# Layer 0's last stage in a written order: last gate group, first GLA weights and norm

## The chip, the cores and the metric

The kernel runs on one core of a Trainium2 chip, as one program. The profile names the core's engines: PE (matrix products, with PEld loading its weights), DVE and ACT (element-wise work), POOL, and SP, from which most loads are issued. ACT and POOL issue loads too. Each engine works through its own instructions in order, and waits on semaphores for the others.

The metric is the time of one execution in device microseconds. Times given are medians of several runs.

## The reference, cut to what matters

Two layers on 512 tokens of width 1024, in float32. Each has a mixer, a gated MLP and a per-layer embedding; layer 0's mixer is attention with a short convolution, layer 1's is gated linear attention (GLA). The change lies where layer 0 ends and layer 1 begins:

```python
def _rms_norm(x, gain):
    y = xf * lax.rsqrt(jnp.mean(xf * xf, axis=-1, keepdims=True) + RMS_EPS)
    return y * gain

def _per_layer_embedding(x, p_i, norm, w_gate, w_proj):   # end of layer 0
    gate = jax.nn.sigmoid(_rms_norm(x, norm) @ w_gate)
    return gate * (p_i @ w_proj)                          # added to x

def _gla_mixer(h, w_in, w_gate_up, gate_bias, o_norm, w_out):   # h = _rms_norm(x, mix_norm[1])
    q, k, v, g_lr, og = _split(h @ w_in, GLA_SPLITS)
    log_a = jax.nn.log_sigmoid(g_lr @ w_gate_up + gate_bias) / GLA_GATE_NORMALIZER
    ...
    o = _gla_chunked(heads(q) * GLA_DK ** -0.5, heads(k), heads(v), heads(log_a))
    o = _rms_norm(o, o_norm) * jax.nn.silu(heads(og))
    return o.reshape(b, s, GLA_VAL_DIM) @ w_out
```

## The kernel before

**Layout and arithmetic.** The state x is held transposed in eight tiles `xT[0..7]` of 128 features by 512 tokens. For float32 accuracy, each operand of a large product is split in two: a rounded part (made on ACT by a copy) and the rest (made on DVE by subtraction). A product is then three matmuls: rounded by rounded, and twice rounded by rest. `cut` (L134) does this for weights: `wh` on ACT at L151, `wl` on DVE at L153, or at L158 when other work is recorded between them (`amid`). `mm3_rests_last` (L181) issues for all terms first the two matmuls that need only one operand's rest, and afterwards, in a second pass, the matmul with the other operand's rest.

**End of layer 0, `ple0` (L1382).** The gate product is done in four groups g of 256 output columns, each from seven block products of half size (`product`) that share weights differences (`first_third`, `second`, `fourth` on DVE). PE, DVE and ACT follow a written order here (`manual_schedule`, L1460). A group's gate is finished one group late (`late`): a multiplication by the token norm R, a sigmoid on ACT, a multiplication by the projection of p (`pjb`, L1524, read from a PSUM bank), and an addition to `xT` (`added`, L1449). `enter` (L1412) then makes the split operands of layer 1 (`xg`: x times the gain, rounded on ACT at L113, its rest on DVE at L114), and `squared` (L1451) takes squares on ACT and adds them up in `acc` on DVE (L319). Behind the last group come the weights of the first 368 GLA value columns, in two halves `raws` (L1552 to L1563), the last gate, the last four blocks of x, and `end_norm` (L361): PE turns `acc` (L358), DVE sums it (L367) and scales it (L205), POOL takes the power -1/2 (L206).

**Start of layer 1, `mixer1` (L1752).** `v.step(0)` and `v.step(1)` (L1773) are the value product with those weights, over blocks 0 to 3 and 4 to 7 of x, into four PSUM banks of the kind `ps`. Their results are scaled by the norm when ACT evicts them (L1787, L1788). Sixteen of the columns feed the decay gate: `gate_up` (L1838) loads its weights from ACT's queue and splits them, `turn_low` (L1852) turns the columns, `log_decays` (L1865) makes the log decays on PE, ACT and DVE. `spread` (L371) turns the norm into a tile R for features in rows. `query(w, 0)` (L1806) is the first feature product, also in a `ps` bank, with `turn_low` recorded after six of its eight terms. Its weights (`pair_w`, L1792) are 1 MB, loaded by SP and split by `cut`. The masks of the chunked attention come by one load (L2093) into a weight buffer (`raw`, two buffers in all), and DVE casts them to bytes (L2094).

**What sets the order.** Outside the written stretches a scheduler orders each engine's instructions when the program is built, by priority; `issue_after(i)` keeps what is recorded in it behind instruction i, `high_priority(offset)` moves it ahead. SP's loads stand in one queue. A tile of a pool with n buffers waits until the tile n places before it has been read.

Of the kernel before, what the change touches and what calls it, by code (L numbers as in the profile page):

```python
# [19 lines left out]
P = 128  # L20
S = 512
# [42 lines left out]
class Kernel:  # L64
# [116 lines left out]
    def mm3_rests_last(self, terms, start, stop, weights, **kw):  # L181


        mm = self.nc.tensor.matmul
        begun, left = set(), {}
        for out, lt, rt in terms:
            left[id(out)] = left.get(id(out), 0) + 1
        for out, (lh, ll), (rh, rl) in terms:
            first = start and id(out) not in begun
            begun.add(id(out))  # L190
            mm(out, lh, rh, start=first, stop=False, **kw)  # L191
            lt, rt = (lh, rl) if weights == 0 else (ll, rh)
            mm(out, lt, rt, start=False, stop=False, **kw)  # L193
        for out, (lh, ll), (rh, rl) in terms:
            left[id(out)] -= 1
            lt, rt = (ll, rh) if weights == 0 else (lh, rl)
            end = mm(out, lt, rt, start=False, stop=stop and not left[id(out)], **kw)  # L197
        return end

    def rsqrt(self, out, src, scale):  # L200

        nc = self.nc
        w = src.shape[1]
        t = self.few(w, "rs", 4)
        nc.vector.tensor_scalar(t, src, scale, EPS, op0=ALU.mult, op1=ALU.add)  # L205
        nc.gpsimd.tensor_tensor(out, t, self.mhalf[:, :w], ALU.pow)  # L206

# [153 lines left out]
    def end_norm(self, sums=None):  # L361

        nc = self.nc
        if sums is None:
            ps = self.by_token()
            sums = self.few(NT, "ss")
            nc.vector.tensor_reduce(sums, ps.rearrange("p (t f) -> p t f", f=P), op=ALU.add, axis=AX.X)  # L367
        self.r = self.few(NT, "rtok")
        self.rsqrt(self.r, sums, 1.0 / D)
# [1012 lines left out]
    def ple0(self, fp, both, gain, next_gain):  # L1382
# [29 lines left out]
        def enter(*ms):  # L1412
            for m in ms:
                hl = self.pair(self.fp, "b0", "b1")
                self.split(hl, self.xT[m], next_gain[:, m : m + 1])
                self.xg.append(hl)

# [25 lines left out]
        def sigmoid(s):  # L1443
            nc.scalar.activation(s, s, AF.Sigmoid)
# [15 lines left out]
        with tc.manual_schedule(engines={ET.PE, ET.DVE, ET.Activation}):  # L1460
# [6 lines left out]
            rounded = lambda hl, src, w=S: nc.scalar.activation(hl[0][:, :w], src[:, :w], AF.Copy)  # L1467
            rest = lambda hl, src, w=S: tt(hl[1][:, :w], src[:, :w], hl[0][:, :w].bitcast(F32), ALU.subtract)
            tt(s34[:, left], e[:, left], e[:, right], ALU.subtract)
            rounded(eh, e, H)  # L1470
            rounded(oh, o)
            tt(s12[:, left], e[:, right], o[:, right], ALU.add)
            rest(eh, e, H)
            tt(s12[:, right], s12[:, left], e[:, left], ALU.subtract)
            rounded(ah, s12)
            rest(oh, o)
            rest(ah, s12)
# [3 lines left out]
            copies(X, Y, bank)  # L1481
            tt(s34[:, right], o[:, left], s12[:, right], ALU.subtract)
# [5 lines left out]
            for g in range(groups):  # L1488
# [18 lines left out]
                copy(X[:, right], Y[:, left])  # L1507
                if late:
                    summed(gates[:, 1], Yb, mb)
# [8 lines left out]
                if not ends:  # L1518
                    raw, ev, od = following
                    plain = self.cut_blocks(raw[:, :, :P])  # L1520
                if late:
                    sigmoid(gates[:, 1])
                    for c in range(2):
                        tt(gates[:, c], gates[:, c], pjb[c], ALU.mult)  # L1524
                if not ends:
                    first_third(ev, od)
                product(X[:, right], t13, 1, x["s3"], False, g > 0)
                copy(Y[:, right], X[:, right])
                if ends:
                    added(before, gates)  # L1530
                    pjs.append(proj(2 * g + 1))
                    squared(before)
                    enter(0, 1, 2, 3)
# [33 lines left out]
        self.end_norm()  # L1567
# [184 lines left out]
    def mixer1(self):  # L1752
        nc, a, tc = self.nc, self.a, self.tc
        xg, r = self.xg, self.r
        w_in = a["gla_w_in"][0].rearrange("(k p) n -> p k n", p=P)
        tok = lambda k, t: (xg[k][0][:, t * P : (t + 1) * P], xg[k][1][:, t * P : (t + 1) * P])
        with tc.tile_pool(name="m1", bufs=1) as mp:
# [5 lines left out]
            class Values:  # L1763
# [9 lines left out]
                def step(v, i):  # L1773
# [15 lines left out]

            qT, kT = [None] * GH, [None] * GH  # L1790
# [4 lines left out]
            def feature(w, c, amid=None):  # L1795
                ps = self.ps()
# [305 lines left out]
            R = self.spread()  # L2102
            w = pair_w(0)
            query(w, 0, turn_low)
# [126 lines left out]
```

## Time and profile before

| | us |
|---|---|
| median of 3 runs | 1208.24 (1206.25 to 1208.59) |
| the profiled execution | 1207.74 |
| its span, first to last instruction | 1206.0 |
| PE busy in the span | 1189.8 |
| DVE busy | 995.2 |
| ACT busy | 692.8 |
| granted PE clock, mean | 0.996 |

A row of a timeline gives the start and the duration in us from the span's start, then engine, line, operation, out<-in with their shapes, the count of merged instructions, and in brackets how long the engine was idle before it and what ended that. A row of the waits gives who waited for whom: us in total, times, longest. A row of windows gives the length of a stretch, then the busy time of PE, weight load, DVE, ACT and POOL with their counts, the granted clock of PE (1.00 is full), the share of the DMA engines and GB/s. L12 is line 12 of the kernel; a helper's line stands for all who call it.

### The profile page before, as it was taken

What the parts mean: (1) busy time and instruction counts of PE and PEld (TensorE: products, weight loads), DVE (VectorE), ACT (ScalarE), POOL (GpSimd) and SP (SyncE); (2) the same over time, 40 slices, a digit from 0 to 9 for tenths busy, and PEclk for the clock granted to TensorE, in tenths of its full rate; (3) what the DMA queues carried; (4) which work ended last, traced back from release to release, by engine and by line L of the source; (5) the groups of instructions that cost most, each with busy time, mean ns of one, the idle gap of its engine ahead of it and who ended that gap; (6) DMA issues with size and microseconds to landing.
All of it is one profiled execution on the core that took longest, in us unless ns stands there. A gap on an engine that the chain in (4) does not pass through costs nothing.

```text
span 1206.0 us, 20223 instructions
## 1 busy us (share of the span) xinstructions
PE 1189.8 (99%) x8218; PEld 1081.3 (90%) x8218; DVE 995.2 (83%) x1593; ACT 692.8 (57%) x1137; POOL 45.9 (4%) x64
## 2 busy tenths in 40 slices
PE   9999999999999999999799999999999999999998
PEld 8877789999999889889688988889999999888887
DVE  6786687898999986989769876687989999988595
ACT  7466556656565654755563565555565656645374
POOL 2600000000000000000100000000000000000000
PEclk9999999999999999999899999999999999999999
DMA  7232222333332433222231322223333333423601
GB/s 222 74 100 74 73 88 71 110 102 109 103 106 88 156 123 97 97 70 86 89 93 47 94 71 70 87 70 106 106 106 106 102 109 96 140 88 97 207 2 70
DMA packets 112928, 117.76 MB, mean 98 GB/s; under 512 B 2840, under 2 KB 107858, under 8 KB 112836
## 3 DMA queue, kind: packets, MB, share of 16 engines
q1 hardware_dynamic: 112000, 115.88, 29.8%
q8 instruction: 64, 1.05, 0.4%
q0 software_dynamic: 560, 0.42, 0.3%
q14 instruction: 28, 0.23, 0.1%
q10 hardware_dynamic: 276, 0.18, 0.1%
HBM read 114.37 MB, written 2.10 MB: 97 GB/s over the span
## 4 chain that ended last, share of the span: by engine, by line
PE 85%; DVE 10%; ACT 3%; issue 1%; DMA 1%; POOL 0%; ACTq 0%; DVEq 0%; POOLq 0%
PE ps L177 8%; PE ps L178 8%; PE ps L179 8%; PE pa L179 6%; PE pa L178 6%; PE pa L177 6%; PE ps L912 5%; PE ps L914 5%; PE ps L913 5%; PE ps L191 4%; PE ps L193 4%; PE ps L197 4%; PE pa L912 2%; PE pa L914 2%; PE pa L913 2%; DVE wl L860 1%
## 5 line engine op out<-in xcount | busy, mean ns | idle before, releaser
L153 DVE TENSOR_TENSOR wl<-raw,wh 128x1024 fp32r<-128x1024 f32 (+4 forms) x140 | 160.8, 1151 | 38.4 <-ACT wh L151 34.9
L151 ACT ACTIVATE wh<-raw 128x1024 fp32r<-128x1024 f32 (+4 forms) x142 | 140.8, 996 | 70.0 <-PE ps L178 28.5
L857 ACT ACTIVATE wh<-raw 128x1024 fp32r<-128x1024 f32 x90 | 95.7, 1064 | 127.5 <-DVE raw L884 79.8
L975 DVE SCALAR_TENSOR_TENSOR zt<-z,vfa,zt 128x510 f32<-128x510 f32 (+1 forms) x176 | 131.1, 746 | 0.3
L860 DVE TENSOR_TENSOR wl<-raw,wh 128x1024 fp32r<-128x1024 f32 x90 | 110.1, 1223 | 18.8 <-ACT wh L857 17.9
L179 PE MATMUL pa<-b,wl 128*128 128x256 f32 x352 | 97.3, 276 | 0.1
L179 PE MATMUL pa<-a,wl 128*128 128x256 f32 x352 | 97.3, 276 | 0.0
L177 PE MATMUL pa<-b,wh 128*128 128x256 f32 x352 | 97.2, 276 | 0.0
L178 PE MATMUL pa<-a,wh 128*128 128x256 f32 x352 | 97.2, 276 | 0.0
L177 PE MATMUL pa<-a,wh 128*128 128x256 f32 x352 | 97.2, 276 | 0.0
L178 PE MATMUL pa<-b,wh 128*128 128x256 f32 x352 | 97.2, 276 | 0.0
L191 PE MATMUL ps<-b,wh 128*128 128x512 f32 (+1 forms) x200 | 77.6, 391 | 5.9 <-ACT wh L151 5.9
L973 ACT ACTIVATE zt<-z,vfb 128x512 f32<-128x512 f32 x88 | 71.4, 811 | 18.2 <-DVE z L965 8.8
L193 PE MATMUL ps<-b,wh 128*128 128x512 f32 (+1 forms) x200 | 76.2, 384 | 0.0
L179 PEld LDWEIGHTS pa<-b,wl 128*128 128x128 f32 x352 | 66.1, 188 | 0.3 <-DVE wl L153 0.3
L178 PEld LDWEIGHTS pa<-a,wh 128*128 128x128 f32 x352 | 66.1, 188 | 0.0
L178 PEld LDWEIGHTS pa<-b,wh 128*128 128x128 f32 x352 | 66.1, 188 | 0.0
L177 PEld LDWEIGHTS pa<-b,wh 128*128 128x128 f32 x352 | 66.1, 188 | 0.0
L177 PEld LDWEIGHTS pa<-a,wh 128*128 128x128 f32 x352 | 66.1, 188 | 0.0
L179 PEld LDWEIGHTS pa<-a,wl 128*128 128x128 f32 x352 | 66.1, 188 | 0.0
L912 PE MATMUL ps<-four,wh 128*128 128x256 f32 x232 | 64.6, 279 | 0.0
L914 PE MATMUL ps<-four,wl 128*128 128x256 f32 x232 | 64.1, 276 | 0.0
(530 smaller groups left out, 3708.6 us busy)
## 6 DMA issues: line engine op xcount, KB each, us to landing
raw<-in_ffn_w_up_dram SPq DMA_DIRECT2D x42, 1024.0 KB, 5.0
raw<-in_ffn_w_down_dram SPq DMA_DIRECT2D x13, 1024.0 KB, 5.1
raw<-in_hy_w_in_dram SPq DMA_DIRECT2D x8, 1024.0 KB, 5.2
raw<-in_gla_w_in_dram SPq DMA_DIRECT2D x8, 1024.0 KB, 5.1
raw<-in_ffn_w_down_dram SPq DMA_DIRECT2D x8, 768.0 KB, 4.8
raw<-in_ple_w_gate_dram SPq DMA_DIRECT2D x6, 1024.0 KB, 5.6
raw<-in_hy_w_out_dram SPq DMA_DIRECT2D x16, 256.0 KB, 4.2
raw<-in_gla_w_out_dram SPq DMA_DIRECT2D x4, 1024.0 KB, 5.0
```

What stands on the lines that cost most here:

```text
L151: nc.scalar.activation(hv, v, AF.Copy)
L153: self.rest_cut = nc.vector.tensor_tensor(lv, v, hv.bitcast(F32), ALU.subtract)
L177: mm(out, lh, rh, start=start, stop=False, **kw)
L178: mm(out, lh, rl, start=False, stop=False, **kw)
L179: mm(out, ll, rh, start=False, stop=stop, **kw)
L191: mm(out, lh, rh, start=first, stop=False, **kw)
L193: mm(out, lt, rt, start=False, stop=False, **kw)
L857: nc.scalar.activation(h, src, AF.Copy)
L860: nc.vector.tensor_tensor(l, src, h.bitcast(F32), ALU.subtract)
L912: mm(out, wh, xh, start=first and j == 0, stop=False, **kw)
L914: mm(out, wl, xh, start=False, stop=j == ND // 2 - 1, **kw)
L975: nc.vector.scalar_tensor_tensor(out=y[:, tap:], in0=z[:, : S - tap], scalar=w[:, f : f + 1], in1=y[:, tap:], op0=ALU.mult, op1=ALU.add,)
```

## The change

In the compiled program the instructions of PE, SP, POOL, DVE and ACT before layer 0's last stage are the same. What the edit does:

- *First group.* The sum form of the first pair (`ah`) is rounded, and its rest taken, in two halves, the second behind the copies.
- *Middle groups.* The multiplication of the first gate half by its projection stands ahead of the rest of the next plain weights.
- *Last group.* `enter` is divided in `rounded_x` (ACT) and `rest_x` (DVE), and `squared` in `square` (ACT) and `sums` (DVE). Blocks 0 and 1 are rounded ahead of the second sigmoid, blocks 2 to 7, the squares, the last gate and the additions in two written lists, between the roundings and the rests of each half of the value weights.
- *Norm.* `end_norm` is issued after the first pass of `v.step(1)`, where the scheduler put the transposes in the middle of that pass before; `rsqrt` returns its DVE instruction.
- *First query.* Its weights are issued after that instruction, its product takes a `pa` bank, and `spread` is recorded with `turn_low` after six of the eight terms.
- *Masks.* Two loads into tiles of the kind `sq`, with two casts.

In the program as built, SP has the first mask load between the two loads of value weights; ACT has both roundings of the first query weights directly behind the last rounding of x and ahead of the five loads of the gate weights, and the two roundings of the first key weights ahead of L1872; on DVE the orders in the first half of layer 1 differ too (one scan, L1898, stands later). PE has the same instructions; the transposes named here, R's and the turned columns' stand elsewhere. From the third head of layer 1 on the orders are as before.

```diff
@@ -181 +181 @@
-    def mm3_rests_last(self, terms, start, stop, weights, **kw):
+    def mm3_rests_last(self, terms, start, stop, weights, amid=None, **kw):
@@ -193 +193,4 @@
-            mm(out, lt, rt, start=False, stop=False, **kw)
+            end = mm(out, lt, rt, start=False, stop=False, **kw)
+        if amid:
+            with self.tc.issue_after(end.ins), self.tc.high_priority(offset=200):
+                amid()
@@ -205 +208 @@
-        nc.vector.tensor_scalar(t, src, scale, EPS, op0=ALU.mult, op1=ALU.add)
+        scaled = nc.vector.tensor_scalar(t, src, scale, EPS, op0=ALU.mult, op1=ALU.add)
@@ -206,0 +210 @@
+        return scaled
@@ -369 +373 @@
-        self.rsqrt(self.r, sums, 1.0 / D)
+        self.norm_scaled = self.rsqrt(self.r, sums, 1.0 / D)
@@ -1412 +1416 @@
-        def enter(*ms):
+        def rounded_x(*ms):
@@ -1415 +1419 @@
-                self.split(hl, self.xT[m], next_gain[:, m : m + 1])
+                nc.scalar.activation(hl[0], self.xT[m], AF.Copy, scale=next_gain[:, m : m + 1])
@@ -1417,0 +1422,17 @@
+        def rest_x(*ms):
+            for m in ms:
+                h, l = self.xg[m]
+                nc.vector.scalar_tensor_tensor(
+                    out=l, in0=self.xT[m], scalar=next_gain[:, m : m + 1], in1=h.bitcast(F32),
+                    op0=ALU.mult, op1=ALU.subtract,
+                )
+        def square(m):
+            sq = spare()
+            nc.scalar.activation(sq, self.xT[m], AF.Square)
+            return sq
+        def sums(*sqs):
+            for sq in sqs:
+                tt(self.acc, self.acc, sq, ALU.add)
@@ -1467,2 +1488,3 @@
-            rounded = lambda hl, src, w=S: nc.scalar.activation(hl[0][:, :w], src[:, :w], AF.Copy)
-            rest = lambda hl, src, w=S: tt(hl[1][:, :w], src[:, :w], hl[0][:, :w].bitcast(F32), ALU.subtract)
+            whole = slice(0, S)
+            rounded = lambda hl, src, c=whole: nc.scalar.activation(hl[0][:, c], src[:, c], AF.Copy)
+            rest = lambda hl, src, c=whole: tt(hl[1][:, c], src[:, c], hl[0][:, c].bitcast(F32), ALU.subtract)
@@ -1470,2 +1492 @@
-            rounded(eh, e, H)
-            rounded(oh, o)
+            rounded(eh, e, left)
@@ -1473 +1494,4 @@
-            rest(eh, e, H)
+            rounded(ah, s12, left)
+            rest(eh, e, left)
+            rounded(oh, o)
+            rest(ah, s12, left)
@@ -1475 +1498,0 @@
-            rounded(ah, s12)
@@ -1477 +1499,0 @@
-            rest(ah, s12)
@@ -1481,0 +1504,2 @@
+            rounded(ah, s12, right)
+            rest(ah, s12, right)
@@ -1507,0 +1532,2 @@
+                if ends:
+                    rounded_x(0, 1)
@@ -1518,4 +1544,2 @@
-                if not ends:
-                    raw, ev, od = following
-                    plain = self.cut_blocks(raw[:, :, :P])
-                if late:
+                times_pj = lambda c: tt(gates[:, c], gates[:, c], pjb[c], ALU.mult)
+                if ends:
@@ -1524,2 +1548,8 @@
-                        tt(gates[:, c], gates[:, c], pjb[c], ALU.mult)
-                if not ends:
+                        times_pj(c)
+                        rest_x(c)
+                else:
+                    raw, ev, od = following
+                    plain = self.cut_blocks(raw[:, :, :P], True, (lambda: times_pj(0)) if late else None)
+                    if late:
+                        sigmoid(gates[:, 1])
+                        times_pj(1)
@@ -1532,2 +1561,0 @@
-                    squared(before)
-                    enter(0, 1, 2, 3)
@@ -1555,11 +1583,30 @@
-            before, (Xb, Yb, mb), pjb = late
-            gates = both()
-            ws = [self.cut(raws[0], "a", amid=lambda: (tt(gates[:, 0], Xb, R, ALU.mult), summed(gates[:, 1], Yb, mb)))]
-            for c in range(2):
-                sigmoid(gates[:, c])
-                tt(gates[:, c], gates[:, c], pjb[c], ALU.mult)
-            added(before, gates)
-            enter(4, 5)
-            ws.append(self.cut(raws[1], "a"))
-            enter(6, 7)
-            squared(before)
+            final, (Xb, Yb, mb), pjb = late
+            sqs = []
+            def behind_first_roundings():
+                rounded_x(2, 3)
+                rest_x(2, 3)
+                sqs.extend(square(2 * before + c) for c in range(2))
+                rounded_x(4, 5)
+                ends = both()
+                summed(ends[:, 1], Yb, mb)
+                sigmoid(ends[:, 1])
+                tt(ends[:, 0], Xb, R, ALU.mult)
+                sigmoid(ends[:, 0])
+                return ends
+            def behind_second_roundings():
+                for c in (1, 0):
+                    times_pj(c)
+                added(final, gates)
+                rest_x(4, 5)
+                sums(*sqs)
+                sqs[:] = [square(2 * final + c) for c in range(2)]
+                rounded_x(6, 7)
+                rest_x(6, 7)
+                sums(*sqs)
+            held = []
+            ws = [self.cut(raws[0], "a", amid=lambda: held.append(behind_first_roundings()))]
+            gates = held[0]
+            ws.append(self.cut(raws[1], "a", amid=behind_second_roundings))
@@ -1567 +1613,0 @@
-        self.end_norm()
@@ -1754 +1800 @@
-        xg, r = self.xg, self.r
+        xg = self.xg
@@ -1783 +1829,2 @@
-                    self.mm3_rests_last(terms, i == 0, i == 1, 1)
+                    norm = self.end_norm if v.given and i else None
+                    self.mm3_rests_last(terms, i == 0, i == 1, 1, norm)
@@ -1785 +1832 @@
-                        rt = r[:, t : t + 1]
+                        rt = self.r[:, t : t + 1]
@@ -1789,0 +1837 @@
+            spread_r = []
@@ -1796 +1844 @@
-                ps = self.ps()
+                ps = self.pa() if amid else self.ps()
@@ -1809 +1857 @@
-                    out=o, in0=feature(w, h % 2, amid), scalar=float(GDK**-0.5), in1=R, op0=ALU.mult, op1=ALU.mult
+                    out=o, in0=feature(w, h % 2, amid), scalar=float(GDK**-0.5), in1=spread_r[0], op0=ALU.mult, op1=ALU.mult
@@ -2092,3 +2140,8 @@
-            mf = self.raw(7, P)
-            nc.sync.dma_start(mf, a["cst_m"].rearrange("p (a b) -> p a b", b=P))
-            nc.vector.tensor_copy(msk, mf)
+            def masks():
+                for c in (slice(0, 4), slice(4, 7)):
+                    mf = self.sp.tile([P, S + 64], F32, tag="sq", name=self.nm("mf"), bufs=2)
+                    mf = mf[:, :S].rearrange("p (a b) -> p a b", b=P)[:, : c.stop - c.start]
+                    nc.sync.dma_start(mf, a["cst_m"].rearrange("p (a b) -> p a b", b=P)[:, c])
+                    nc.vector.tensor_copy(msk[:, c], mf)
@@ -2102,3 +2155,5 @@
-            R = self.spread()
-            w = pair_w(0)
-            query(w, 0, turn_low)
+            with tc.issue_after(self.norm_scaled.ins):
+                w = pair_w(0)
+            masks()
+            query(w, 0, lambda: (spread_r.append(self.spread()), turn_low()))
+            R = spread_r[0]
```

More of the change, by code (lines that the diff above doesn't have):

```diff
@@ L1466, in ple0 @@
             parts = lambda hl: [(hl[0][:, c], hl[1][:, c]) for c in HALVES]
-            rounded = lambda hl, src, w=S: nc.scalar.activation(hl[0][:, :w], src[:, :w], AF.Copy)
-            rest = lambda hl, src, w=S: tt(hl[1][:, :w], src[:, :w], hl[0][:, :w].bitcast(F32), ALU.subtract)
+            whole = slice(0, S)
+            rounded = lambda hl, src, c=whole: nc.scalar.activation(hl[0][:, c], src[:, c], AF.Copy)
+            rest = lambda hl, src, c=whole: tt(hl[1][:, c], src[:, c], hl[0][:, c].bitcast(F32), ALU.subtract)
             tt(s34[:, left], e[:, left], e[:, right], ALU.subtract)
-            rounded(eh, e, H)
+            rounded(eh, e, left)
+            tt(s12[:, left], e[:, right], o[:, right], ALU.add)
+            rounded(ah, s12, left)
+            rest(eh, e, left)
             rounded(oh, o)
-            tt(s12[:, left], e[:, right], o[:, right], ALU.add)
-            rest(eh, e, H)
+            rest(ah, s12, left)
             tt(s12[:, right], s12[:, left], e[:, left], ALU.subtract)
-            rounded(ah, s12)
             rest(oh, o)
-            rest(ah, s12)
             forms.append(dict(e1=parts(eh)[0], o1=parts(oh)[0], o2=parts(oh)[1], s1=parts(ah)[0], s2=parts(ah)[1],
```

## The prediction

> **What bounds the kernel now.** I read the page first, then the waits of PE, then PE in order of time around the two long ones, then the granted clock there, then ACT, DVE and the DMA queues in the same stretch, and last DVE further on, in layer 1.
>
> ```profile
> span 1206.0 us, 20223 instructions
> PE 1189.8 (99%) x8218; PEld 1081.3 (90%) x8218; DVE 995.2 (83%) x1593; ACT 692.8 (57%) x1137; POOL 45.9 (4%) x64
> PE ps L191 <- ACT wh L151: 8.1, 2, 5.9
> PE pa L912 <- ACT ps L1436: 0.7, 1, 0.7
> PE pa L191 <- DVE zt L1524: 0.6, 1, 0.6
> ```
>
> PE is busy 99% of the span, so 1206.0 - 1189.8 = 16.2 us is all that can be won without less work on PE. Half of it, 8.1 us, lies in two waits for a rounding of weights (columns: in total, times, longest), and all three rows lie in the stage that changes.
>
> ```profile
> 573.84 0.39 PE L197 MATMUL ps<-b,wl 128*128 128x256 f32 x2
> 576.49 0.43 PE L191 MATMUL ps<-wh,b 128*128 128x368 f32 x1 [2.26 <-ACT wh L151]
> 581.97 2.84 PE L197 MATMUL ps<-wl,b 128*128 128x368 f32 x16
> 584.65 0.33 PE L191 MATMUL ps<-wh,b 128*128 128x368 f32 x1
> ...
> 593.14 0.60 PE L376 MATMUL pa<-cf,rtok 128*128 128x128 f32 x4
> 599.60 0.79 PE L191 MATMUL ps<-b,wh 128*128 128x512 f32 x1 [5.86 <-ACT wh L151]
> 604.22 1.54 PE L197 MATMUL ps<-b,wl 128*128 128x512 f32 x6
> 605.60 0.60 PE L1855 MATMUL pa<-cf,glr 128*16 128x128 f32 x4
> 606.98 0.62 PE L197 MATMUL ps<-b,wl 128*128 128x512 f32 x2
> 596.60:599.60 3.00, 0.00 (x1) 0.01 (x1) 1.13 (x3) 2.98 (x7) 0.00 (x0) 0.50 0.00 0
> 599.60:603.40 3.80, 3.80 (x9) 3.03 (x10) 3.47 (x3) 1.84 (x2) 0.00 (x0) 0.50 0.10 9
> ```
>
> Start, duration, what ended the idle time. At 573.84 the last group ends; at 576.49 the first GLA values begin: step 0 until 584.65, step 1 until 593.14. Then PE turns the norm round (L376), idles until 599.60, and runs the first query product. The second 16 matmuls of step 0 take 584.65 - 581.97 = 2.68 us, 0.1675 each. The last two rows are windows (length, busy time of PE, weight load, DVE, ACT and POOL, granted clock, DMA): from 3 us into the long idle until 603.4 the clock is 0.50. The 2.26 us idle left no such trace: 32 matmuls in 581.97 - 576.49 = 5.48 us is full pace. At full pace six 512-wide matmuls take 605.60 - 604.22 = 1.38 us, 0.23 each.
>
> ```profile
> 570.59 0.37 ACT L1528 COPY ps<-ps 128x256 f32<-128x256 f32 x1
> 573.18 2.55 ACT L113 ACTIVATE b<-xT,vec 128x512 fp32r<-128x512 f32 x4
> 575.64 1.51 ACT L151 ACTIVATE wh<-raw 128x736 fp32r<-128x736 f32 x2
> 590.69 1.35 ACTq L1843 DMA_DIRECT2D wgu<-in_gla_w_gate_up_dram  x3
> 592.07 0.79 ACTq L1845 DMA_DIRECT2D wgu<-in_gla_gate_bias_dram  x2
> 595.48 0.63 ACT L1847 ACTIVATE wgs<-wgu 64x512 fp32r<-64x512 f32 x1 [1.16 <-DMA wgu<-in_gla_w_gate_up_dram]
> 597.99 0.59 ACT L378 COPY R<-pa 128x512 f32<-128x512 f32 x1
> 598.46 2.98 ACT L151 ACTIVATE wh<-raw 128x1024 fp32r<-128x1024 f32 x3
> 608.72 2.07 ACT L1872 ACTIVATE F<-pa 128x512 f32<-128x512 f32 x4 [0.21 <-PE pa L1870]
> ```
>
> Both waits are waits for a place in ACT's queue. The values' roundings (575.64) stand behind four roundings of x (573.18). The query's (598.46) stand behind the five loads of the gate weights (590.69), a wait for their landing (1.16 us before 595.48), the evictions and R. In the window from 596.6 ACT is busy 2.98 of 3.00 us, until 598.46 with work for which PE doesn't wait. **PE's wait is made by order, not by throughput.**
>
> **The change part by part.** The order of the built program decides, and I walk through it with these durations, on the time axis of before.
>
> ```profile
> 544.47 1.23 DVE L860 TENSOR_TENSOR wl<-raw,wh 128x1024 fp32r<-128x1024 f32 x1 [0.65 <-ACT wh L857]
> 569.33 0.69 DVE L1441 TENSOR_TENSOR zt<-zt,R 128x512 f32<-128x512 f32 x1
> 571.32 1.29 DVE L1449 TENSOR_TENSOR xT<-xT,zt 128x512 f32<-128x512 f32 x2
> 574.12 2.73 DVE L114 SCALAR_TENSOR_TENSOR b<-xT,vec,b 128x512 fp32r<-128x512 f32 x4
> 578.69 1.75 DVE L158 TENSOR_TENSOR wl<-raw,wh 128x736 fp32r<-128x736 f32 x2
> 587.08 1.49 DVE L319 TENSOR_TENSOR acc<-acc,so 128x512 f32<-128x512 f32 x2
> 591.23 1.01 POOL L206 TENSOR_TENSOR rtok<-rs,mhalf 128x4 f32<-128x4 f32 x1
> 623.89 0.42 DVE L1904 TENSOR_TENSOR F<-kT,qT 128x256 f32<-128x256 f32 x1
> ```
>
> *Middle groups.* The first product with the projection now stands ahead of the weights' rest on DVE, in its 0.65 us idle before 544.47, so the bank for which PE waited 0.6 us is read 0.6 us sooner: **gain 0.6** (bounds 0 and 0.6). The second group's case was not waiting before.
>
> *First group.* One of the 512-wide forms is cut in two, and the second half goes behind two copies: one 256-wide instruction more on each of ACT and DVE (0.42 us, last row) in a chain that ends in the squares that PE's transposes need. The V product still waits for the same copies, so 0.7 us stays. Loss between 0 and 0.42; I take **0.2**, since half of an extra instruction falls into idle time.
>
> *Last group to values.* On ACT the value weights now come right behind two roundings of x and the last copy, so they are rounded by 572.5 (570.59 + 0.37 + 1.51) and PE needs them at 573.84 + 0.23 = 574.07: the 2.26 us wait, with the drain 576.49 - 574.07 = 2.4, goes. What is late next is DVE. From 569.93 it has, until the last square is summed: two products with the projection (0.6 each, pitch of L1449), eight rests of x (0.67), four adds to x (0.6), the three sums of the last gate (1.9), two weight rests (0.85), two more products (0.6), four sums of squares (0.74): 16.7 us, and 0.5 of waits for ACT, so 587.1. PE needs the rests of x one by one from 574.2 and, in step 1, from 582.3 on, and the sum for the transposes at 574.07 + 5.36 + 2.68 + 5.36 = 587.5. That is a margin of 0.4 us after 17 us of DVE without a gap; the rest of x's seventh block, needed at 584.95, has none. The third of the four weight rests comes at 587.9, 0.1 late. Step 1 so ends near 590.6 against 593.14: **gain 2.5**.
>
> *Mask loads.* Two smaller loads instead of one, the first of them ahead of the second value weights on SP's queue. It waits for a PE product of the last group that is over before DVE frees the buffer of these weights, so it costs nothing; if it waited longer, that load, and then step 1, would be queued behind it. Freed of the masks, the buffer takes the query weights some 6 us sooner. The two casts stand ahead of the norm's sums on DVE, hidden because ACT, which uses the norm, is issuing loads then. On POOL two memsets of scores move ahead of the gate weights' memset, which waits for PE's transposes anyway.
>
> *First query.* Its weights are rounded on ACT right behind the last x (585.9), its rest comes behind the norm's scaling (591.4, needed 593.4), its bank is free. R's transposes and the turn of the gate follow 18 matmuls later. Before, 593.14 to 606.98 + 0.46 = 607.44 is 14.3 us; without idle time and at full clock it is 24 x 0.23 + 2 x 0.36 = 6.2. Gain 8.1, if no new wait comes. One does: ACT reaches the loads of the gate weights when it has the second half of the query weights, which wait for the rest at 587.9, so it issues from 589.05 to 591.2 (1.35 + 0.79); the norm's power (1.01) is there by 591.3. In before the first use came 595.48 - 590.69 = 4.8 after the first issue; so 593.85 now, and R 597.99 - 595.48 = 2.5 later, 596.4. The last of the four columns that are turned is ready just before R, near 596.1, and PE wants it at 595.6: loss 0.5. **Gain 7.6**.
>
> ```profile
> raw<-in_gla_w_in_dram SPq DMA_DIRECT2D x4, 1024.0 KB, 5.1
> wgu<-in_gla_w_gate_up_dram ACTq DMA_DIRECT2D x3, 32.0 KB, 4.4
> ```
>
> The landing is the least sure number: SP now issues the next 1 MB load (key weights) at 588.8, 0.3 us ahead. At best the first use comes 4.4 after the first issue, 0.4 sooner; at worst the gate's rows start only when that load has landed, 588.8 + 5.1 = 593.9, and take their 4.4 again: 598.3, 4.5 later. I take the 4.8 of before, since 32 KB are little beside either end. [...] No row here shows the two side by side.
>
> *Layer 1.* The rows that follow say how much PE can keep.
>
> ```profile
> 616.27 2.48 DVE L1881 SCALAR_TENSOR_TENSOR la<-pa,F 128x512 f32<-128x512 f32 x4 [1.38 <-ACT F L1878]
> 619.93 2.33 DVE L1898 TENSOR_TENSOR_SCAN G<-run,la 128x512 f32<-128x512 f32 x2
> 654.35 0.69 DVE L1816 TENSOR_TENSOR kT<-ps,R 128x512 f32<-128x512 f32 x1
> 655.09 0.42 PE L191 MATMUL ps<-wh,b 128*128 128x336 f32 x1
> 625.00:650.00 25.00, 25.00 (x185) 20.34 (x184) 24.78 (x65) 11.01 (x21) 0.00 (x0) 1.00 0.20 57
> ```
>
> DVE is full here (24.78 of 25.00 us), and PE's matmul at 655.09 starts 0.05 after the key that DVE evicts until 655.04. So PE keeps only what DVE gains. Two copies of the turned columns, 0.6 each like R's, end near 598.1; then come two roundings of key weights (2.0, both ahead of L1872 now), so L1872 starts at 600.05 against 608.72, and L1881 at 607.6: 8.7 earlier. Until L1904 one scan less (2.33/2) stands on DVE, so that starts 9.8 earlier; between it and the key stand a scan more and one 256-wide product less, so the key comes 9.1 earlier. PE would be 2.5 + 7.6 = 10.1 earlier: **1.0 is given back**.
>
> Sum: 0.6 - 0.2 + 2.5 + 7.6 - 1.0 = 9.5 us. Against the profiled execution, 1207.74 us (span 1206.0 and 1.74 around it), 1198.2; that execution is 0.5 below the median of 1208.24. I say **1198.5 us**.
>
> **The rivals.**
> *DVE or the gate chain runs late.* With 17 us of DVE behind one another and a margin of 0.4, some 0.1 more per hand-over between ACT and DVE (ten of them), or gate rows 1 to 4 us late beside the key load, makes PE wait 1.5 to 4 us more at the transposes or in layer 1. For it: DVE's zero margins. Against: each operand in the walk but two has over 0.4. Time 1199.5 to 1202.7.
>
> *Full gain.* DVE order in layer 1 also changes, and the key may come earlier than counted; then 1.0 and the 0.5 stay: 1196.7.
>
> *The query still stalls*, since its weights' rest or landing is late by over 5 us: half of the 7.6 stays, 1203 to 1206. Against: weights rounded 4.7 us ahead of use. A wait up to about 2.3 us costs only itself, one of 5.9 also 1.9 of slow clock. [...]
>
> *Slower: the log decays.* The two roundings of key weights now stand ahead of L1872 on ACT, for a load that SP issues only when DVE has done the last value rest. Where this load lands after 606.7 (608.72 less 2.0), layer 1's DVE work starts later than before, and every microsecond beyond is lost one for one: landing at 610 would give about 1211. For it: the load is queued on SP behind a wait for DVE. Against: 588.8 + 5.1 = 593.9 is 12.8 us ahead.
>
> That the change doesn't do what it says is out: the built order has it.
>
> **How the numbers follow.** Forecast 0.55 (own range 1196.5 to 1200); late chain 0.20; full gain 0.08; query stall 0.10; log decays 0.05; nothing measurable 0.02. Within 0.2% (2.4 us) of before counts as no change, about what a measurement here can tell: the query stall has some of that. Faster 0.91, same 0.04, slower 0.05. The range takes in the upper end of the landing and the lower of all unknowns (0 for each loss): 1195.5 to 1202.8, which leaves out most of the last three cases.
>
> **What would show it.** Right: PE without idle time ahead of the values; L358's transposes behind all 32 first matmuls with under 0.5 us of wait; the query's first matmul within 0.3 us of the last value; clock 1.00 throughout; waits of 0.3 to 1 us at the fourth turned column and at the key in layer 1. Wrong: a wait over 1 us on DVE's acc or x rests, the gate's rows landing later than 595, a clock of 0.50 in this stretch, or the key on DVE less than 8 us earlier.

## The result, and the profile after

The changed kernel takes 1199.10 us (median of 4 runs, 1198.45 to 1200.29) against 1207.78 of the kernel before beside it (4 runs, 1206.25 to 1208.59): a ratio of 0.9931, 95% interval 0.9914 to 0.9948. The forecast was 1198.5. The profiled execution took 1199.61, its span 1197.3.

The head of the changed kernel's page, and then its waits of PE (in total, times, longest):

```profile
span 1197.3 us, 20223 instructions
PE 1187.8 (99%) x8218; PEld 1079.0 (90%) x8218; DVE 995.0 (83%) x1595; ACT 692.4 (58%) x1138; POOL 46.2 (4%) x64
```

```profile
PE pa L1903 <- ACT glr L1834: 1.1, 2, 0.9
PE ps L191 <- DVE kT L1864: 0.8, 1, 0.8
PE pa L916 <- ACT ps L1457: 0.7, 1, 0.7
PE pa L362 <- DVE acc L323: 0.3, 1, 0.3
```

Both waits for a rounding (8.1 us) are gone, and so is the 0.6 at the projection's bank. The 0.7 at the first group stays. Three waits are new: 1.1 at the turned gate columns, 0.8 at a key of layer 1, 0.3 at the transposes of layer 0's own norm, behind the first group. So 8.7 us of waits went and 2.2 came. The timeline of PE, and one window of it:

```profile
573.12 0.39 PE L200 MATMUL ps<-b,wl 128*128 128x256 f32 x2
573.35 0.33 PE L191 MATMUL ps<-wh,b 128*128 128x368 f32 x1
584.35 0.33 PE L191 MATMUL ps<-wh,b 128*128 128x368 f32 x1
584.76 0.44 PE L193 MATMUL ps<-wh,b 128*128 128x368 f32 x1
587.39 0.60 PE L362 MATMUL pa<-cf,acc 128*128 128x128 f32 x4
590.51 0.40 PE L191 MATMUL pa<-b,wh 128*128 128x512 f32 x1
595.69 0.28 PE L1903 MATMUL pa<-cf,glr 128*16 128x128 f32 x1 [0.23 <-ACT glr L1834]
597.08 0.28 PE L1903 MATMUL pa<-cf,glr 128*16 128x128 f32 x1 [0.88 <-ACT glr L1834]
598.34 0.39 PE L191 MATMUL ps<-b,wh 128*128 128x512 f32 x1
```

```profile
563.00:600.00 37.00, 35.80 (x217) 32.15 (x216) 30.89 (x46) 23.64 (x42) 4.33 (x7) 1.00 0.39 121
```

The last group ends with the matmuls at 573.12, the values start at 573.35 without idle time, the query product at 590.51 right behind them, and the second query product at 598.34. The clock in the window is 1.00. The timeline of ACT, POOL and DVE there:

```profile
584.44 1.04 ACT L151 ACTIVATE wh<-raw 128x1024 fp32r<-128x1024 f32 x1
589.34 1.48 ACTq L1891 DMA_DIRECT2D wgu<-in_gla_w_gate_up_dram  x3
592.69 0.27 ACT L1834 ACTIVATE glr<-ps,rtok 128x16 f32<-128x16 f32 x1 [3.98 <-POOL rtok L209]
594.84 0.63 ACT L1895 ACTIVATE wgs<-wgu 64x512 fp32r<-64x512 f32 x1 [0.83 <-DMA wgu<-in_gla_w_gate_up_dram]
596.76 0.27 ACT L1834 ACTIVATE glr<-ps,rtok 128x16 f32<-128x16 f32 x1
590.74 1.92 POOL L209 TENSOR_TENSOR rtok<-rs,mhalf 128x4 f32<-128x4 f32 x1 [1.43 <-DVE rs L208]
590.56 2.36 DVE L153 TENSOR_TENSOR wl<-raw,wh 128x1024 fp32r<-128x1024 f32 x2
645.99 0.69 DVE L1864 TENSOR_TENSOR kT<-ps,R 128x512 f32<-128x512 f32 x1
```

The first rounding of query weights starts at 584.44, 6 us ahead of its use. The new chain that PE meets is on ACT: gate loads from 589.34, their first use at 594.84 behind 0.83 us of wait for the rows, and the fourth gate column evicted only behind that (596.76).

### The profile page after: what moved, and what is told of

It is laid out like the page before. It is cut to its first block, busy times and chain, and to the rows that moved or that the text cites. A ratio compares the mean times of both kernels' runs of the same rounds, so it can differ in the third digit from the quotient of the medians.

```text
span 1197.3 us, 20223 instructions
## 1 busy us (share of the span) xinstructions
PE 1187.8 (99%) x8218; PEld 1079.0 (90%) x8218; DVE 995.0 (83%) x1595; ACT 692.4 (58%) x1138; POOL 46.2 (4%) x64
## 4 chain that ended last, share of the span: by engine, by line
PE 84%; DVE 10%; ACT 3%; DMA 1%; issue 1%; POOL 0%; ACTq 0%; POOLq 0%; DVEq 0%
PE ps L177 8%; PE ps L178 8%; PE ps L179 8%; PE pa L178 6%; PE pa L179 6%; PE pa L177 6%; PE ps L916 5%; PE ps L918 5%; PE ps L917 5%; PE ps L191 4%; PE ps L193 4%; PE ps L200 4%; PE pa L916 2%; PE pa L918 2%; PE pa L917 2%; DVE wl L864 1%
## 5 line engine op out<-in xcount | busy, mean ns | idle before, releaser
L153 DVE TENSOR_TENSOR wl<-raw,wh 128x1024 fp32r<-128x1024 f32 (+3 forms) x138 | 158.9, 1153 | 36.4 <-ACT wh L151 33.2
L191 PE MATMUL ps<-b,wh 128*128 128x512 f32 (+1 forms) x192 | 73.1, 384 | 0.0
L193 PE MATMUL ps<-b,wh 128*128 128x512 f32 (+1 forms) x192 | 72.1, 378 | 0.0
```

The costliest lines, as they stand in the source:

```text
L153: self.rest_cut = nc.vector.tensor_tensor(lv, v, hv.bitcast(F32), ALU.subtract)
L193: end = mm(out, lt, rt, start=False, stop=False, **kw)
```

## Experiments: which part carries the gain

Each undoes one part of the changed kernel. Ratios are to the kernel before in the same series; they are what to compare by, since the changed kernel itself took 1199.10 us in its first series and 1200.07 in another. *The masks* in one load into a weight buffer again, at their old place ahead of the query weights:

```diff
-                for c in (slice(0, 4), slice(4, 7)):
-                    mf = self.sp.tile([P, S + 64], F32, tag="sq", name=self.nm("mf"), bufs=2)
...
+                mf = self.raw(7, P)
+                nc.sync.dma_start(mf, a["cst_m"].rearrange("p (a b) -> p a b", b=P))
```

> Only the masks go back to one load into a weight buffer; everything else as in the changed kernel. My theory (the first query product's gain comes from the load of its weights, which the masks held back): SP's load of the query weights waits again for the second value weights' rest (588.4 in the changed kernel's profile) and lands near 593.5, the roundings come behind the evictions near 597.5, and PE idles 7 to 8 us before the query product, with a clock of 0.50 behind it: 1206.5 to 1209. Rival (the position of the roundings on ACT and the free bank make the gain, the masks are an accessory): at most 1 us, so 1199 to 1200.

Measured 1208.47 us (10 runs, ratio 1.0002, 0.9993 to 1.0011). Its one new wait, its timeline of ACT, two windows, and SP's loads of feature weights, first in the changed kernel and then here:

```profile
PE pa L191 <- ACT wh L151: 8.1, 1, 8.1
```

```profile
597.60 2.95 ACT L151 ACTIVATE wh<-raw 128x1024 fp32r<-128x1024 f32 x3
```

```profile
590.57:592.60 2.03, 0.00 (x1) 0.00 (x0) 0.00 (x0) 0.88 (x4) 1.01 (x1) 1.00 1.07 370
592.70:602.80 10.10, 4.08 (x10) 3.21 (x11) 4.51 (x5) 5.76 (x10) 0.00 (x0) 0.50 0.42 129
```

```profile
578.19 24.68 SPq L120 DMA_DIRECT2D raw<-in_gla_w_in_dram  x4
588.34 13.12 SPq L120 DMA_DIRECT2D raw<-in_gla_w_in_dram  x3
```

The load of the query weights, the first of each row, is issued at 588.34 instead of 578.19, the roundings come behind the evictions again, PE idles 8.1 us, and the clock is 0.50 for 10.1 us. With the new order of the last group and the free bank in place, the kernel is no faster than before: only without the masks in that buffer do the query weights come early, and without that what the rest of the change wins turns into idle time at the query.

*The last group* in its old order, all else as changed:

```diff
-                if ends:
-                    rounded_x(0, 1)
...
+                    squared(before)
+                    for m in range(4):
+                        rounded_x(m)
+                        rest_x(m)
...
-            ws.append(self.cut(raws[1], "a", amid=behind_second_roundings))
+            for m in (4, 5):
+                rounded_x(m)
+                rest_x(m)
+            ws.append(self.cut(raws[1], "a"))
...
```

> Only the written order of the last group goes back to the old one (whole splits of x, squares at the end); the first and middle groups, the norm behind the first pass, the masks and the bank stay. My theory: the values wait again 2.3 us for their rounded weights behind four roundings of x, and step 1 ends 2 to 3 us later: 1201 to 1202.5. Rival (the norm's transposes behind all 32 first products make the gain of the value steps, and the order only moves the idle time): under 0.7 us, so below 1199.8.

Measured 1201.58 (4 runs, 1201.29 to 1202.26; ratio 0.9945, 0.9930 to 0.9960). The start of the values on PE, and two windows:

```profile
576.22 0.43 PE L191 MATMUL ps<-wh,b 128*128 128x368 f32 x1 [2.42 <-ACT wh L151]
```

```profile
573.80:576.22 2.42, 0.01 (x1) 0.01 (x1) 2.42 (x5) 2.42 (x5) 0.00 (x0) 1.00 0.00 0
577.10:580.40 3.30, 3.30 (x13) 3.30 (x12) 3.27 (x6) 2.50 (x5) 0.00 (x0) 0.50 0.00 0
```

The wait of before is back, so the order is what removed it, and not the new place of the norm, which this run keeps. The clock is 0.50 in the window that follows, though PE had resumed, which costs up to 1.7 us more; the 1.1 us at the gate columns is not there. The profiled span is 2.9 us longer, 2.42 + 1.7 - 1.1 = 3.0; by the ratios it is 1.7 us, with intervals that overlap.

*The query product* in a `ps` bank again:

```diff
-                ps = self.pa() if amid else self.ps()
+                ps = self.ps()
```

> Only the first query product goes back to a ps bank. My theory: its first matmul waits for the eviction of the first values (593.4 instead of 590.5), 2.9 us; the 1.1 us at the turned columns and part of the 0.8 us at the key are then gone, so 1.0 to 1.8 us net: 1200.1 to 1200.9. Rival A (bank without effect since the values are evicted in time): 1199.1. Rival B (nothing is taken back): 1202.

Measured 1202.76 (5 runs, 1202.05 to 1204.34; ratio 0.9960, 0.9946 to 0.9974). The wait and two windows:

```profile
PE ps L191 <- ACT vt L1835: 2.8, 1, 2.8
```

```profile
590.58:592.90 2.32, 0.01 (x1) 0.00 (x0) 2.27 (x3) 0.28 (x2) 1.92 (x1) 1.00 1.07 379
593.00:596.30 3.30, 2.91 (x7) 2.33 (x8) 0.00 (x0) 1.99 (x6) 0.00 (x0) 0.50 0.72 208
```

The wait is as expected, the time is not: at 0.50 the clock costs up to half of the 3.3 us again, which I had not counted. The span is 2.6 us longer than the changed kernel's, and by the ratios it is 3.5 us.

*The middle groups*, and in a second kernel *the first group*, as before:

```diff
-                    plain = self.cut_blocks(raw[:, :, :P], True, (lambda: times_pj(0)) if late else None)
+                    plain = self.cut_blocks(raw[:, :, :P])
                     if late:
+                        times_pj(0)
```

```diff
-            rounded(ah, s12, left)
...
+            rounded(ah, s12)
             rest(oh, o)
+            rest(ah, s12)
```

> Only the middle groups go back: the product with the projection behind the rest of the plain weights. Forecast: PE waits 0.6 us again for the bank, and the first value matmul starts at 573.95 instead of 573.35. Rival (the wait is gone for another reason): 573.35.

> Only the first group's halves go back to one 512-wide form. The changed kernel's first value matmul starts at 573.35. Forecast (one instruction more on ACT and DVE costs 0.2): it starts at 573.15 here. Rival (the halves win time, since the V product's rest is ready sooner): 573.5 to 574.0.

One execution each: 1200.07 and 1198.40. The starts (574.54 and 573.19) decide little, since the changed kernel, run again, starts its values at 573.57 instead of 573.35. The waits do decide. In the run with the old middle groups stands

```profile
PE pa L191 <- DVE zt L1544: 0.6, 1, 0.6
```

and in the run with the whole form the 0.3 at L362 is not listed, which the changed kernel has. So the one gains 0.6, and the other costs 0.3 (0.2 in the changed kernel run again). The new places of the norm and of R in PE's order were not undone by themselves.

## Experiments: where the rest of the forecast went

The power of the norm took 1.92 us instead of the 1.01 that I had taken over. DVE's subtraction of query weights (590.56) ran beside it. One instruction more, a copy of the norm, holds DVE back until the power is done:

```diff
+                seen = nc.vector.tensor_copy(self.few(NT, "seen"), self.r)
+            with tc.issue_after(seen.ins):
                 w = pair_w(0)
```

> One instruction more: DVE copies the norm (128x4) ahead of the rests of the query weights, so that these don't run beside POOL's power; all else stands as in the changed kernel. Theory 1 (the power took 1.92 instead of 1.01 us since DVE's subtraction ran beside it, but the fourth turned column waits for the landing of the gate rows, behind which its eviction stands): the power takes 1.0 us, the evictions start 0.9 us earlier, the waits at the turned columns stay at 0.9 to 1.1, time within 0.3 of 1199.1. Theory 2 (the power is what makes the columns late): the waits go and the time is 1198.0. Theory 3 (no relation between DVE and POOL): the power stays at 1.9.

Measured 1210.96 (10 runs; ratio 1.0023, 1.0014 to 1.0033), 12 us above the changed kernel, which no theory had. The power on the timeline, the column wait, the page's head, and one group of matmuls (busy us, mean ns):

```profile
596.99 1.01 POOL L209 TENSOR_TENSOR rtok<-rs,mhalf 128x4 f32<-128x4 f32 x1 [1.43 <-DVE rs L208]
```

```profile
PE pa L1903 <- ACT glr L1834: 0.7, 1, 0.7
```

```profile
PE 1199.7 (99%) x8218; PEld 1090.9 (90%) x8218; DVE 996.5 (82%) x1596; ACT 691.6 (57%) x1138; POOL 45.4 (4%) x64
```

```profile
L916 PE MATMUL ps<-four,wh 128*128 128x256 f32 x232 | 65.9, 284 | 0.0
```

It is 1.01, and the column wait hardly moved, as theory 1 said. PE's busy time is what grew, from 1187.8 to 1199.7 in the same 8218 matmuls. The copy went to a tile of a kind of its own: two buffers of 128 x 8 floats, so everything allocated behind stands 64 bytes further on each partition. The same instructions, with the copy in an existing kind:

```diff
-                seen = nc.vector.tensor_copy(self.few(NT, "seen"), self.r)
+                seen = nc.vector.tensor_copy(self.few(NT, "ss"), self.r)
```

> The same instructions as in the run before with the copy of the norm, but the copy goes to a tile kind that exists already, so that no tile of the kernel changes its address (the run before had 64 bytes more ahead of the large tiles, and its matmuls of 256 columns took 280 to 284 ns instead of 276 to 279 in the MLPs). Theory 1 (the 12 us of that run come from the addresses): power 1.0 us, waits at the turned columns about 0.7 us, time 1198.5 to 1199.3. Theory 2 (they come from the copy or the wait in DVE's queue): about 1211 again.

Measured 1200.83 (4 runs, 1200.45 to 1202.53; ratio 0.9944, 0.9929 to 0.9959), above the range of theory 1 and far from the 1211 of theory 2. The same group, the head and the timeline of ACT:

```profile
L916 PE MATMUL ps<-four,wh 128*128 128x256 f32 x232 | 64.7, 279 | 0.0
```

```profile
PE 1188.7 (99%) x8218; PEld 1080.0 (90%) x8218; DVE 995.0 (83%) x1596; ACT 693.0 (58%) x1138; POOL 45.7 (4%) x64
```

```profile
592.79 0.28 ACT L1834 ACTIVATE glr<-ps,rtok 128x16 f32<-128x16 f32 x1 [3.57 <-DMA wgu<-in_gla_gate_bias_dram]
```

So some 10 us of that run (1210.96 against 1200.83) go with these 64 bytes: 284 ns instead of 279 for such a matmul of the MLPs, and 1 to 6 ns more in their other groups of 256 columns. All engines have the same instructions in the same order in the two runs, and 5.7 us of the loss stand ahead of the copy, for ACT starts the first rounding of the query weights at 590.69 in the one and at 584.95 in the other; so it is not the copy. The power alone wins nothing: the evictions start at 592.79, behind gate loads that were issued until 592.66 in this execution, and PE still waits 0.9 us for the fourth column.

Next, the rows themselves. Their tile is of the kind F, cleared ahead of PE's transposes, and ACT issues the loads ahead of the second rounding of the query weights, which only the second query needs:

```diff
-                w = self.sp.tile([P, S], F32, tag="acc", name="wgu", bufs=1)
+                w = new()
...
+            if k and behind:
+                with self.tc.issue_after(behind), self.tc.high_priority(offset=400):
+                    nc.scalar.activation(hv, v, AF.Copy)
```

> The gate weights go to a tile of the kind F, whose clearing does not wait for PE's transposes, and their loads stand ahead of the second rounding of the query weights on ACT (that half is for the second query product). Theory 1 (the landing of the gate rows sets the turned columns and the log decays): loads issued from 587.5, landed by 592.5, no wait at the turned columns, log decays about 1 us earlier, time 1197.8 to 1198.3. Theory 2 (the late power sets them): unchanged, 1199.1.

Measured 1200.12 (4 runs, 1199.09 to 1200.67; ratio 0.9932, 0.9919 to 0.9946). The timeline of ACT, and the wait:

```profile
587.57 2.47 ACTq L1895 DMA_DIRECT2D F<-in_gla_w_gate_up_dram  x3
593.32 0.63 ACT L1899 ACTIVATE wgs<-F 64x512 fp32r<-64x512 f32 x1 [1.29 <-DMA F<-in_gla_gate_bias_dram]
593.86 0.25 ACT L1838 ACTIVATE glr<-ps,rtok 128x16 f32<-128x16 f32 x1
```

```profile
PE pa L1907 <- ACT glr L1838: 1.2, 3, 0.6
```

The loads are issued 1.8 us earlier and used 1.5 earlier, but now the first use stands ahead of all four columns, which wait with it. The ratio is that of the changed kernel (0.9931), as theory 2 said, but its reason is not shown: the columns wait for the rows, not for the power. With the norm's copy and the columns ahead as well:

```diff
+                    for t in range(NT if i and n > vn else 0):
+                        rt = self.r[:, t : t + 1]
+                        with tc.high_priority(offset=300):
+                            nc.scalar.activation(glr[:, t, :], v.pss[t][:, vn:n], AF.Copy, scale=rt)
```

> Both cures together (gate loads ahead, the norm's copy ahead of the rests), and the four evictions of the gate columns ahead of the other evictions. Theory (the rest of the loss is this chain): no wait at the turned columns, key wait under 0.4 us, log decays 1.5 us earlier, 1197.2 to 1197.8. Rival (DVE in layer 1 does not follow, the key's wait grows by what is won): 1198.2 to 1199.1.

Measured 1199.61 (5 runs, 1198.97 to 1202.12; ratio 0.9932, 0.9920 to 0.9945), slower than the theory and its rival had it. The timeline, and a window:

```profile
596.05 0.63 ACT L1902 ACTIVATE wgs<-F 32x512 fp32r<-32x512 f32 x1 [1.47 <-DMA F<-in_gla_w_gate_up_dram]
600.88 1.93 PE L1924 MATMUL pa<-gT,wgs 96*128 96x512 f32 x4 [2.35 <-DVE gT L1917]
```

```profile
601.20:604.50 3.30, 3.30 (x9) 2.53 (x9) 2.61 (x3) 3.28 (x6) 0.00 (x0) 0.50 0.01 2
```

The columns no longer wait. But the last rows were there only at 596.05, and on ACT the evictions, R and the roundings of the turned columns (until 600.11) stand behind them. DVE's rest of the turned columns had to wait for these, and PE waited 2.35 us for that rest at the projection, which the scheduler had put three matmuls earlier; the clock is at 0.50 behind it. This execution was the slowest of the five (1202.12 us). In three of the others the mean clock was 1.000, which leaves no room for such a drop; whether PE waited as long there is not recorded. Last, the loads on SP's queue ahead of the key weights, on ACT all else as changed, and a second kernel with the norm's copy and the columns ahead too:

```diff
-                    nc.scalar.dma_start(w[u : u + GR, :], a["gla_w_gate_up"][0])
+                    nc.sync.dma_start(w[u : u + GR, :], a["gla_w_gate_up"][0])
```

> The gate weights go to a tile of the kind F, and their five loads are issued by SP ahead of the load of the key weights, no longer by ACT. Theory 1 (on ACT's queue the gate rows landed beside the 1 MB of key weights, 5.0 to 7.6 us after their first issue; ahead of that load they land sooner): landing under 4.8 us after the first issue and ahead of the evictions, no wait at the fourth turned column, log decays about 1 us earlier, time 1197.7 to 1198.4. Theory 2 (the landing takes 5 us or more whatever stands beside it): rows at 593 or later, and the time within 0.5 of the changed kernel's.

> As the run before, and the norm's copy ahead of the rests of the query weights (power without DVE beside it), and the evictions of the gate columns ahead. Theory: rtok 0.9 us sooner, log decays 1.5 to 1.9 us earlier than in the changed kernel, PE waits at the columns 0 and at the key under 0.4: 1197.0 to 1197.8. Rival (the key on DVE does not follow): its wait grows to over 1.2, 1198 to 1199.

> The changed kernel again, beside the two runs before and the kernel before: 1198.5 to 1199.7, gate rows landing 4.6 to 5.7 us after their first issue, 0.8 to 1.1 us of wait at the turned columns and 0.7 to 0.8 at the key.

All three in one series: 1200.70 (1199.42 to 1201.53; ratio 0.9935, 0.9923 to 0.9947), 1199.33 (1198.10 to 1199.68; 0.9922, 0.9908 to 0.9935) and, for the changed kernel again, 1200.07 (1198.69 to 1200.50; 0.9929, 0.9917 to 0.9942), 5 runs each. The last is above what I expected, with 1.5 us of wait at the columns in its profile. The landing of the gate rows (the view of their tile), first in the changed kernel, then on SP's queue, and there the timeline of PE:

```profile
DMA to landing us min/median/max: 4.6/5.1/5.1
```

```profile
DMA to landing us min/median/max: 2.5/2.6/2.7
```

```profile
599.17 1.22 PE L1918 MATMUL pa<-gT,wgs 96*128 96x512 f32 x4 [1.92 <-DVE gT L1911]
```

Ahead of the 1 MB load a gate load takes 2.6 us, behind its issue 5.1. That is the order and not the queue: on ACT's queue, but ahead of that load, its three rows took 3.1 in median (the first run with the loads moved). The landing is as theory 1 had it and the columns no longer wait, and still nothing is won: PE now waits 1.92 us at the projection for DVE's rest of the turned columns, since the scheduler put the projection four matmuls earlier. With both cures, on the timeline and among the waits:

```profile
599.16 1.22 PE L1920 MATMUL pa<-gT,wgs 96*128 96x512 f32 x4 [0.93 <-DVE gT L1913]
```

```profile
PE ps L191 <- DVE kT L1866: 0.6, 1, 0.6
```

The wait at the projection is 0.93, and the median lies 0.7 below the changed kernel's, with overlapping runs. Whether it is faster stays open. Its key wait (0.6) is neither the theory's nor the rival's. Written by hand, PE's place for the projection might give the 0.9; that was not tried.

## Why the prediction was right, step by step

*What bounds it.* PE's order-made waits were the gain: no work left PE (8218 matmuls in both), and its idle time fell from 16.2 us to 1197.3 - 1187.8 = 9.5.

*Middle and first groups.* 0.6 won and 0.2 to 0.3 lost, as forecast (0.6, 0.2).

*Last group to values.* The 2.4 us went, and came back when the order was undone. The zero margin showed where it was named: the rest of the seventh block came 0.24 us late (584.76 instead of 584.52, one step of 0.1675 behind 584.35). From the first value to the query it took 590.51 - 573.35 = 17.16 us, against 16.5 in my walk. So from the end of the last group to the query 1.9 us were won (593.14 - 573.84 = 19.30 before, 590.51 - 573.12 = 17.39 after), not 2.5.

*First query.* 598.34 - 590.51 = 7.8 us against 14.3 before: 6.5 won, not 7.6. The wait at the columns was 1.1 instead of 0.5. The other 0.5 is listed as no wait: 7.83 - 1.11 = 6.72 us, where the walk had 6.2 without idle time. PE's drain at the two waits (0.16 us at the values' wait of before: 576.49 - 574.07 = 2.42, of which 2.26 idle), for which the walk had no term, is likely part of it; here it was not measured by itself. Behind the wait stands the landing of the gate rows: first use 594.84 - 589.34 = 5.5 us after the first issue, where I had taken over 4.8. What the DMA queues moved in the changed kernel, from 589.0 to 592.7 (one row) and from 592.7 to 594.4 (two), shows why (packets, MB, share of the 16 engines; q1 has the 1 MB loads, q10 the gate rows):

```profile
q1 hardware_dynamic: 914, 0.94, 82.1%
q1 hardware_dynamic: 147, 0.13, 41.4%
q10 hardware_dynamic: 100, 0.10, 17.5%
```

No packet of the rows is moved for 3.4 us after their first issue, until nine tenths of the key weights have been. In the kernel before it is the same: the rows, issued from 590.69, move from 593.57 on, with the end of a 1 MB load that SP issued at 589.26. So my sentence that no row shows the two side by side was wrong, and the 4.8 had such a load in it. Counted from that load's issue, the first use came 595.48 - 589.26 = 6.2 us later before and 594.84 - 588.43 = 6.4 after; with this count my walk would have had 588.8 + 6.2 = 595.0 instead of 593.85. The rows came behind nearly all of the load and did not share with it from the start. My worst case had them start behind the load, but then counted a landing of 4.4 us that had this waiting in it already. What holds them back is not shown.

*The power.* I priced it at 1.01 from before, where DVE was not beside it. It took 1.92 us beside the subtraction and 1.01 when DVE waited for it; the windows above have the same, 1.92 with the query in a `ps` bank again, where DVE is busy 2.27 of 2.32 us, and 1.01 with the old masks, where DVE is idle. That DVE was held back is not shown, for both its subtractions ran in their usual 1.22 us. Why the power takes longer is not shown either. The miss cost little by itself, since the rows came later still: without it the column wait stayed at 0.7 and 0.9 us.

*Layer 1.* The key is 654.35 - 645.99 = 8.4 us earlier, where 9.1 and the 0.4 of the first groups make 9.5. ACT starts the log decays' first step (L1872, now L1920) at 600.93 instead of 608.72, 7.8 us earlier and not 8.7 + 0.4 = 9.1: the late gate chain again. PE waits 0.8 at the key, near the 1.0 that was to be given back.

*Rivals.* "DVE or the gate chain runs late" is the one that came true in part: 0.6 us at the columns. My sentence that a wait up to about 2.3 us costs only itself held for 2.26 us and was no rule: behind waits of 2.42, 2.81 and 2.35 us (the last group in its old order, the `ps` bank, gate loads, norm's copy and columns ahead on ACT) came 3.4 us at 0.50 each.

In sum the spans differ by 1206.0 - 1197.3 = 8.7 us, where 9.5 was forecast. The waits account for 8.7 - 2.2 = 6.5 of it, and the 3.8 us at half clock behind the long wait of before for 1.9 more. That the sum came so near is in part luck. Up to the end of the last group 0.7 us were won (573.84 - 573.12; 0.4 forecast), from there to the query 1.9 (2.5), at the query 6.5 (7.6), and 0.4 was given back behind it (1.0): two terms were too high, and the other two made up for half of that.

## What to carry to other kernels

When a wait is for a place in an engine's queue, look at what keeps the data from being there earlier: here a smaller load that borrowed a large buffer decided where 1 MB of weights stood in the order. Price a moved instruction by what will run beside it, not by its row from before (the power took 1.92 us beside DVE's subtraction and 1.01 without), and count with a long PE wait the clock that it may cost: here the waits of 2.35 to 8.15 us cost 3.4 to 10.2 us at 0.50, one of 2.26 us none. Here a cure that moved one wait won nothing as long as the order behind it stayed. Look also at what a duration from the old trace already contains: the landing that I took over had a large load in it.

## What the runs showed of the hardware

*Addresses.* With all that is allocated behind the copy's tile 64 bytes further on, matmuls of the MLPs took up to some 2% longer (284 against 279 ns in the group shown), 11.0 us of PE's busy time (1199.7 - 1188.7), with the same instructions. One pair of programs showed it; which of the moved operands matters, and why, was not tried.

*The clock.* PE's idle times of 2.35 us (gate loads, norm's copy and columns ahead on ACT), 2.42 (the last group in its old order) and 2.81 (the `ps` bank) each came with 3.4 us at 0.50, the 5.86 us of the kernel before with 6.8, and the 8.15 us of the run with the old masks with 10.2. The 2.26 us of the kernel before came with none (the clock is 1.00 from 576.5 to 584.0), and behind the 1.92 us at the projection, with the loads on SP's queue, PE's next 512-wide matmuls start 0.23 us apart, as at full pace. In the run with the old last group the drop came (577.1) after PE had resumed (576.22). What decides whether the clock drops, and for how long, is not shown.
